# The norm stage of a decoder layer: normed rows multiplied one step later, with g read from PSUM

## The chip, the cores and the metric

The kernel runs on one core of one Trainium2 chip. The metric is device time in microseconds (us): 1281.83 us is the median of three runs of the kernel before (1281.49 to 1283.53). Below, a number such as 586.76 beside an instruction is its start, counted in us from the start of the profiled span.

## What is computed

One hybrid decoder layer on x of 1024 rows by 1024 columns, all in float32. After two groups of attention heads the layer does this, and the change lies in these lines (and in the first norm, which uses the same helper):

```
x = x + einsum('bse,ed->bsd', mixed, w_out)      # output projection and residual
h = rms_norm(x, ffn_norm_g)                      # x * rsqrt(mean(x*x) + eps) * g, row by row
g = einsum('bsd,df->bsf', h, w_gate)
u = einsum('bsd,df->bsf', h, w_up)
x = x + einsum('bsf,fd->bsd', silu(g) * u, w_down)
return rms_norm(x, final_norm_g)
```

Each float32 product is made of three TensorE products of "high" and "low" parts, so every operand is split: ScalarE (ACT) writes the rounded high part, and VectorE (DVE) or GpSimd (POOL) writes the rest, the low part. The gate and up products are made by a Strassen scheme (seven block products in place of eight) on 2 by 2 blocks, which needs sums of blocks of h (named T1 to T4 beside the plain blocks 11, 12, 21, 22) and sums of weight blocks (s1, s2 and two more).

## The kernel before

The 1024 rows are eight row tiles of 128. The stage that the change touches is the loop over `order = (7, 6, 5, 4, 0, 1, 2, 3)` (L812 to L843), the **norm stage**; it lies between the attention and the gate and up products, and step n treats row tile order[n]. It stands in a block whose order is written out by hand: within `manual_schedule` TensorE (PE), DVE, ACT and POOL take their instructions in program order. The DMA queue of SyncE (SP) and all that lies outside the block is ordered by a planner, from its own estimates of time, when the program is built, and the planner may put such instructions between those of the block.

One step n of the loop, engine by engine in program order:
- PE: twelve matmuls of the output projection for columns 0 to 511 (L602, called from L819, tile pso), the transposes of the normed rows of step n - 2 (L757; eight for the lower rows 4 to 7, four for the upper rows), then twelve matmuls for columns 512 to 1023.
- DVE: the residual sum of the first half (L823); the subtractions of step n - 2 on the transposed rows (L765 or L774 into a temporary place, L748 for the low part); in four of the steps the low part of a weight sum (L710, "ol<-temps"); the residual sum of the second half (L823); then the mean of squares plus eps (L136, one column); then the normed rows, x times r times g (L830, tile xn, 1024 columns).
- ACT: copies and high parts of step n - 2 (L762, L744, L764), the high part of a weight sum (L709), the sum of squares of the new rows (L135, with its accumulator read).
- POOL: the power of minus one half (L137, one column), the low part of T3 of step n - 2 (for the upper rows: the subtraction of L779 and the low part of T1), then weight sums by `plan` (L724, L805, L807).

So in the old order L830 of step n stands on DVE after L137 of step n and ahead of the first sum of step n + 1. There is one tile of two temporary places, `temps`: place 0 for T3 or T1, place 1 for weight sums; below the loop both serve T4. The vector g (`gb2`) lies in SBUF, repeated over the 128 partitions. The transposes take their PSUM banks in turn from two pools of two banks, ps_p ("pj") and ps_t ("t").

Below the loop, still by hand (L862 to L882, here **the tail**): four products whose operands are ready, kept in PSUM (`held`), with the transposes of row tiles 2 and 3 and the second column halves of row tiles 0 to 3 between them, and the splits of all these (`first_half`, `first_half_below`). The block ends there. The first product of the stage behind it is `strassen_first`'s product of a11 with block 11 (L957, matmuls on L855, "pst<-11h,oh"), which takes a bank of ps_p. One bank of ps_p is held by the last of the four held products until later.

`rstd_of` (L133 to L138) is also called for each of the eight row tiles of the first norm, at the start of the kernel (0 to 42 us).

## Time and profile before

| | us |
|---|---|
| median of three runs | 1281.83 |
| the profiled execution, its own time | 1281.52 |
| its span | 1279.8 |
| PE busy | 1230.0 (96%) |
| DVE busy | 865.0 (68%) |
| ACT busy | 572.2 (45%) |
| POOL busy | 715.0 (56%) |

The profile is one execution. Each engine takes its instructions in order; a time in brackets behind an instruction is how long the engine sat idle before it, with the engine and the line that ended the wait by the semaphores (of several, the one named can be the wrong one). A matmul row of 0.39 us starts some 0.23 us after the one before it: matmuls overlap. The granted TensorE clock is a share of 2.4 GHz, so 0.50 is its lower level, 1.2 GHz.

### The profile page before, as it was taken

To read this page: it belongs to the slowest core of one execution; us is meant where nothing else is said; L and a number is where in the kernel's file an instruction comes from. 1 tells how busy PE (TensorE), PEld (TensorE's weight loads), DVE (VectorE), ACT (ScalarE), POOL (GpSimd) and SP (SyncE) were. 2 spreads that over 40 slices of the span, in tenths; PEclk is the share of its full clock that TensorE was granted. 3 is DMA by queue.
4 is the path that set the end of the run, shared out by engine and by line. 5 is a ranking of instruction groups with operands and counts; after the bars stand their busy time and mean duration, and the time that the engine had idled before them with its cause. 6 is when DMAs were issued, how large, how long until landed. Compare 5 with 4: busy or idle time off the path is not lost.

```text
span 1279.8 us, 18426 instructions
## 1 busy us (share of the span) xinstructions
PE 1230.0 (96%) x6341; PEld 1043.5 (82%) x6341; DVE 865.0 (68%) x1625; ACT 572.2 (45%) x1209; POOL 715.0 (56%) x653
## 2 busy tenths in 40 slices
PE   8999999999999998988699999999999999999997
PEld 7889988987898877876477888888888887788886
DVE  6456767757786778766666655665665668878765
ACT  4345555646684765534443322333332335534334
POOL 2322333233114353344638777778787758999973
PEclk9999999999999998999899999999999999999999
DMA  6231222132103324122123443223333357645313
GB/s 215 69 102 42 71 76 76 30 93 55 42 5 83 107 87 169 46 99 83 33 68 105 155 142 107 88 97 97 122 107 107 99 179 244 220 124 173 100 58 132
DMA packets 93373, 131.42 MB, mean 103 GB/s; under 512 B 7584, under 2 KB 56288, under 8 KB 93280
## 3 DMA queue, kind: packets, MB, share of 16 engines
q1 hardware_dynamic: 91984, 126.32, 31.7%
q10 hardware_dynamic: 1296, 3.94, 0.8%
q8 instruction: 50, 0.82, 0.3%
q14 instruction: 43, 0.35, 0.1%
HBM read 93.75 MB, written 30.18 MB: 97 GB/s over the span
## 4 chain that ended last, share of the span: by engine, by line
PE 79%; POOL 7%; DVE 5%; issue 4%; ACT 2%; DMA 2%; SPq 0%; POOLq 0%; ACTq 0%; DVEq 0%
PE pst L855 31%; PE psd L1076 13%; PE psv L230 6%; PE pv L375 4%; PE pso L602 3%; PE tp L390 3%; PE s L330 2%; PE s L331 2%; POOL unit L1047 1%; PE psq_f1q L293 1%; PE psq_d2q L293 1%; PE psq_f2q L293 1%; PE psq_d3k L293 1%; PE psq_f1k L293 1%; PE psq_f3q L293 1%
## 5 line engine op out<-in xcount | busy, mean ns | idle before, releaser
L1076 PE MATMUL psd<-unit 128*128 128x512 f32 x924 | 212.5, 392 | 3.9 <-DVE x L1088 3.1
L1076 PEld LDWEIGHTS psd<-unit 128*128 128x128 f32 x924 | 174.1, 189 | 42.1 <-DVE x L1088 3.6
L1047 DVE TENSOR_TENSOR unit<-araw,unit 128x512 fp32r<-128x512 f32 x77 | 104.2, 1380 | 32.1 <-ACT unit L1046 20.3
L710 DVE TENSOR_TENSOR ol<-st,oh 128x512 fp32r<-128x512 f32 x84 | 90.7, 1081 | 50.4 <-ACT oh L709 49.1
L709 ACT CAST oh<-st 128x512 fp32r<-128x512 f32 x84 | 51.1, 620 | 152.3 <-POOL st L724 112.5
L334 ACT ACTIVATE pt<-pt,mn 128x896 f32<-128x896 f32 (+7 forms) x128 | 99.4, 777 | 40.3 <-DVE mn L332 38.2
L397 DVE TENSOR_TENSOR pl<-tp,ph 128x512 fp32r<-128x512 f32 (+1 forms) x120 | 75.3, 633 | 45.2 <-ACT ph L396 44.6
L396 ACT CAST ph<-tp 128x512 fp32r<-128x512 f32 (+1 forms) x120 | 64.2, 542 | 63.9 <-PE tp L390 54.1
L978 POOL TENSOR_TENSOR sg<-sg,cc 128x512 f32<-128x512 f32 x44 | 64.9, 1477 | 44.0 <-ACT sg L977 32.6
L710 DVE TENSOR_TENSOR ol<-raw,oh 128x512 fp32r<-128x512 f32 x66 | 66.8, 1013 | 33.1 <-ACT oh L709 33.0
L1046 ACT CAST unit<-araw 128x512 fp32r<-128x512 f32 x77 | 47.4, 620 | 75.0 <-PE psd L1076 33.9
L422 POOL TENSOR_SCALAR_AFFINE_SELECT cb<-cb 128x128 f32<-128x128 f32 x64 | 22.1, 347 | 99.2 <-DVE mn L332 60.6
L984 POOL TENSOR_TENSOR sg<-sg,cc 128x512 f32<-128x512 f32 x40 | 59.4, 1485 | 29.6 <-DVE cc L983 29.5
L709 ACT CAST oh<-raw 128x512 fp32r<-128x512 f32 x66 | 40.8, 618 | 76.3 <-PE pst L855 74.7
L724 POOL TENSOR_TENSOR st<-raw 128x512 f32<-128x512 f32 x42 | 55.4, 1320 | 31.9 <-DMA raw<-in_w_gate_dram 23.0
L394 POOL MEMSET ph<- 128x128 f32 x48 | 9.9, 207 | 106.2 <-PE pv L375 99.8
L390 PE MATMUL tp<-ident,pt 128*128 128x128 f32 x432 | 67.7, 275 | 0.8 <-DVE pt L475 0.4
L127 POOL TENSOR_TENSOR wl<-wr,wh 128x1024 fp32r<-128x1024 f32 x26 | 63.5, 2445 | 1.4
L126 POOL TENSOR_SCALAR wh<-wr 128x1024 fp32r<-128x1024 f32 x26 | 28.8, 1110 | 52.2 <-PE psq_f2k L293 13.1
L390 PEld LDWEIGHTS tp<-ident,pt 128*128 128x128 f32 x432 | 51.7, 142 | 5.8 <-DVE pl L397 1.4
L230 PE MATMUL psv<-wh,hh 128*128 128x256 f32 x192 | 55.0, 287 | 0.1
L230 PE MATMUL psv<-wl,hh 128*128 128x256 f32 x192 | 54.7, 285 | 0.0
(385 smaller groups left out, 3859.8 us busy)
## 6 DMA issues: line engine op xcount, KB each, us to landing
araw<-act_d SPq DMA_DIRECT2D x77, 256.0 KB, 2.7
raw<-in_w_gate_dram SPq DMA_DIRECT2D x24, 512.0 KB, 3.8
raw<-in_w_up_dram SPq DMA_DIRECT2D x24, 512.0 KB, 3.9
wr<-in_w_in_dram SPq DMA_DIRECT2D x22, 512.0 KB, 4.1
act_d<-sa SPq DMA_DIRECT2D x44, 256.0 KB, 2.5
wraw<-in_w_down_dram SPq DMA_DIRECT2D x40, 256.0 KB, 4.3
act_d<-sg SPq DMA_DIRECT2D x33, 256.0 KB, 2.0
xt<-in_x_dram SPq DMA_DIRECT2D x8, 512.0 KB, 5.0
```

The costliest lines, as they stand in the source:

```text
L230: T.matmul(ps[:, :n], hslice(l, dt, tb), r, start=(k == 0), stop=(k == 23))
L293: T.matmul(ps, l[:, dt], r[half][dt // 4][:, dt % 4], start=(k == 0), stop=(k == 23))
L334: A.activation(pt[:, :L], pt[:, :L], AF.Exp, bias=mn[:, nb - 1:nb], scale=-1.0, accum_out=mn[:, 2:3])
L390: T.transpose(tp[:, a * 256 + b * P:a * 256 + (b + 1) * P], pts[b][:, sb * P:(sb + 1) * P], ident)
L396: A.copy(ph[:, o:], tp[:, o:])
L397: V.tensor_sub(pl[:, o:], tp[:, o:], ph[:, o:].bitcast(F32))
L709: A.copy(h, src)
L710: V.tensor_sub(l, src, h.bitcast(F32))
L855: T.matmul(ps, l[:, j], r[:, j], start=(k == 0), stop=(k == 11))
L978: G.tensor_mul(sg, sg, g)
L1047: lo = le.tensor_tensor(u[:, 2 * k + 1], src, u[:, 2 * k].bitcast(F32), ALU.subtract)
L1076: T.matmul(open_banks[i, m], l, r, start=(k == 0 and not top), stop=(k == last), skip_group_check=top)
```

## The change

- `rstd_of`: the mean of squares times 1/D plus eps moves from DVE (`tensor_scalar`) to ACT (`activation` with Copy, scale and bias). This holds for both norms.
- g is copied once, by two ACT copies, into two PSUM banks: one of the pool ps_v (its only one), one of the two of ps_t. The SBUF place of `gb2` then goes to a second tile of two temporary places.
- The normed rows of step n are no longer written at the end of step n but in step n + 1, on DVE behind the first residual sum, as two instructions of 512 columns that read g from PSUM (`normed`). Those of row tile 3 are written in the tail.
- T3 and T1 alternate between places 0 and 2, T4 between 1 and 3.
- The transposes take ps_p, ps_t, ps_p in turn: three banks. The transposes of row tiles 2 and 3 in the tail take ps_t, ps_p where they took ps_t, ps_p by a cycle of three.
- `plan` and the reload of the first weight blocks move one step later (steps 1 to 6 and 7, for 0 to 5 and 6). The SP loads that belong to them follow the same program places.

```
--- before.py
+++ after.py
@@ -133,7 +133,7 @@
     def rstd_of(src, junk, pool):
         ss = pool.tile([P, 2], F32, tag="ss", name="ss", bufs=4)
         A.activation(junk, src, AF.Square, accum_out=ss[:, 0:1])
-        V.tensor_scalar(ss[:, 0:1], ss[:, 0:1], 1.0 / D, EPS, ALU.mult, ALU.add)
+        A.activation(ss[:, 0:1], ss[:, 0:1], AF.Copy, scale=1.0 / D, bias=EPS)
         rstd_of.last = G.tensor_tensor(ss[:, 1:2], ss[:, 0:1], mhalf, ALU.pow)
         return ss[:, 1:2]
 
@@ -731,10 +731,11 @@
     b_op, xns = {}, {}
     r12, r22 = (fa.tile([P, 4, 512], F32, tag="xb", name=f"r{q}2") for q in (1, 2))
     b_op["T3"] = tuple(fa.tile([P, 4, 512], F32R, tag="xb", name="T3" + c) for c in "hl")
-    temps = bp.tile([P, 2, 512], F32, tag="b", name="temps")
+    temps = [bp.tile([P, 2, 512], F32, tag="b", name="temps")]
 
     def temp(k):
-        return temps[:, k].rearrange("p (j t) -> p j t", j=4)
+
+        return temps[k // 2][:, k % 2].rearrange("p (j t) -> p j t", j=4)
 
     def at(x, t):
         c = t % 4 * P
@@ -749,7 +750,7 @@
 
     turn = [0]
 
-    def transposed(t, q, banks=((ps_p, "pj"), (ps_t, "t"))):
+    def transposed(t, q, banks=((ps_p, "pj"), (ps_t, "t"), (ps_p, "pj"))):
         pool, tag = banks[turn[0] % len(banks)]
         turn[0] += 1
         pt = pool.tile([P, 512], F32, tag=tag, name="pt")
@@ -762,28 +763,30 @@
         A.copy(at(r12, t), pvs[0])
         hi_part("22", t, pvs[1])
         A.copy(at(r22, t), pvs[1])
-        V.tensor_sub(temp(0), pvs[1], at(r12, t))
+        t3 = temp(t % 2 * 2)
+        V.tensor_sub(t3, pvs[1], at(r12, t))
         lo_part("22", t, pvs[1], V)
-        hi_part("T3", t, temp(0))
-        return lambda: lo_part("T3", t, temp(0), G)
+        hi_part("T3", t, t3)
+        return lambda: lo_part("T3", t, t3, G)
 
     def first_half(t, pvs):
 
 
         hi_part("11", t, pvs[0])
-        V.tensor_sub(temp(0), at(r12, t), pvs[0])
+        t1 = temp(t % 2 * 2)
+        V.tensor_sub(t1, at(r12, t), pvs[0])
         lo_part("11", t, pvs[0], V)
-        hi_part("T1", t, temp(0))
+        hi_part("T1", t, t1)
 
         def pool():
-            G.tensor_sub(at(r22, t), at(r22, t), temp(0))
-            lo_part("T1", t, temp(0), G)
+            G.tensor_sub(at(r22, t), at(r22, t), t1)
+            lo_part("T1", t, t1, G)
             hi_part("T2", t, at(r22, t))
         return pool
 
     def first_half_below(t, pv):
 
-        t4 = temp(t % 2)
+        t4 = temp(t % 2 * 2 + 1)
         hi_part("21", t, pv)
         V.tensor_sub(t4, pv, at(r22, t))
         lo_part("21", t, pv, V)
@@ -807,8 +810,21 @@
             G.tensor_tensor(temp(1), a11, a21, ALU.subtract)
 
 
-    plan = {0: (0, 0), 1: (0, 1), 2: (0, 2), 3: (1, 0), 4: (1, 1), 5: (1, 2)}
+    plan = {1: (0, 0), 2: (0, 1), 3: (0, 2), 4: (1, 0), 5: (1, 1), 6: (1, 2)}
     order = (7, 6, 5, 4, 0, 1, 2, 3)
+
+    g_at = [pool.tile([P, 512], F32, tag=tag, name="g_at") for pool, tag in ((ps_v, "pv"), (ps_t, "t"))]
+    for nh in range(2):
+        A.copy(g_at[nh], gb2[:, nh * 512:nh * 512 + 512])
+    temps.append(bp.tile([P, 2, 512], F32, tag="b", name="temps"))
+    rs = {}
+
+    def normed(tb):
+        for nh in range(2):
+            cs = slice(nh * 512, nh * 512 + 512)
+            V.scalar_tensor_tensor(xns[tb][:, cs], x2[tb // 2][:, tb % 2, cs], rs[tb], g_at[nh],
+                                   ALU.mult, ALU.mult)
+
     manual = tc.manual_schedule(engines=NORM_MAN)
     manual.__enter__()
     for n, tb in enumerate(order):
@@ -821,13 +837,15 @@
                 t = order[n - 2]
                 pvs = [transposed(t, q) for q in range(2 if t >= 4 else 1)]
             V.tensor_add(xt[:, cs], ps, xa_half(tb, nh))
-            if nh == 0 and n >= 2:
-                late = (second_half if t >= 4 else first_half)(t, pvs)
-            if nh == 0 and plan.get(n - 1, (0, 0))[1]:
-                early[plan[n - 1][0]].append(operand(temp(1)))
+            if nh == 0:
+                if n >= 1:
+                    normed(order[n - 1])
+                if n >= 2:
+                    late = (second_half if t >= 4 else first_half)(t, pvs)
+                if plan.get(n - 1, (0, 0))[1]:
+                    early[plan[n - 1][0]].append(operand(temp(1)))
         xns[tb] = pp.tile([P, D], F32, tag="p", name="xn")
-        r = rstd_of(xt, xns[tb], sm)
-        V.scalar_tensor_tensor(xns[tb], xt, r, gb2, ALU.mult, ALU.mult)
+        rs[tb] = rstd_of(xt, xns[tb], sm)
         if tb >= 4:
             nc.scalar.dma_start(out=x2_d[(tb - 4) * P:(tb - 3) * P, :], in_=xt)
         if n >= 2:
@@ -836,11 +854,11 @@
             early_sum(*plan[n])
         if n == 1:
             b_op["22"] = big("h22h"), big("h22l")
-        if n == 6:
-            w_first[0] = w_blocks(0, 0)
         if n == 5:
             for name in ("11", "T1", "T2"):
                 b_op[name] = tuple(big(name + c) for c in "hl")
+        if n == 7:
+            w_first[0] = w_blocks(0, 0)
 
 
 
@@ -863,6 +881,7 @@
         b_op[name] = tuple(big(name + c) for c in "hl")
     held[0][0] = product(early[0][0], "22", SS)
     pvs = [transposed(2, 0)]
+    normed(3)
     first_half(2, pvs)()
     held[0][1] = product(early[0][1], "T3", SS)
     pvs = [transposed(3, 0)]
@@ -875,7 +894,7 @@
     for t in (0, 1):
         first_half_below(t, pvs[t])
     held[1][1] = product(early[1][1], "T3", PJ)
-    pvs = [transposed(t, 1, (TT, TT, PJ)) for t in (2, 3)]
+    pvs = [transposed(t, 1, (TT, PJ)) for t in (2, 3)]
     a_first.append(operand(w_first[0][2]))
     for t in (2, 3):
         first_half_below(t, pvs[t - 2])
```

## Rows read from the trace of the kernel before

**Rows 1.** The page: the span, and the busy time of the engines.
```profile
span 1279.8 us, 18426 instructions
PE 1230.0 (96%) x6341; PEld 1043.5 (82%) x6341; DVE 865.0 (68%) x1625; ACT 572.2 (45%) x1209; POOL 715.0 (56%) x653
```
**Rows 2.** Busy time by stretch: the stretch and its length, then PE, PE's weight loads, DVE, ACT, POOL (with counts), the granted clock of PE, the DMA share, GB/s. The first stretch is most of the loop, the second the tail.
```profile
570.00:613.00 43.00, 36.85 (x176) 28.46 (x174) 29.69 (x39) 16.89 (x32) 22.38 (x18) 1.00 0.21 66
613.00:642.00 29.00, 17.93 (x75) 13.68 (x74) 19.30 (x25) 13.90 (x25) 18.93 (x14) 0.83 0.09 30
```
**Rows 3.** The timeline of PE from 586 to 642 us, the rows in which it had waited and the last matmul of the loop: start, length, instruction, count, and in brackets the idle time before it and who ended it.
```profile
586.98 1.06 PE L757 MATMUL pt<-ident,xn 128*128 128x128 f32 x8 [1.40 <-DVE xn L830]
...
595.02 1.06 PE L757 MATMUL pt<-ident,xn 128*128 128x128 f32 x8 [1.44 <-DVE xn L830]
...
612.93 0.39 PE L602 MATMUL pso<-w2h,mx 128*128 128x512 f32 x1
...
617.83 0.63 PE L757 MATMUL pt<-ident,xn 128*128 128x128 f32 x4 [1.35 <-DVE xn L830]
...
625.20 0.79 PE L757 MATMUL pt<-ident,xn 128*128 128x128 f32 x4 [3.77 <-DVE xn L830]
...
636.00 1.94 PE L757 MATMUL pt<-ident,xn 128*128 128x128 f32 x8 [2.23 <-DVE 21l L748]
641.49 0.76 PE L855 MATMUL pst<-11h,oh 128*128 128x512 f32 x1 [3.56 <-ACT T4h L744]
```
**Rows 4.** The timeline of DVE over one step of the loop (n = 3), from its first residual sum to that of the next step.
```profile
586.76 0.68 DVE L823 TENSOR_TENSOR x<-pso,x 128x512 f32<-128x512 f32 x1
587.36 0.67 DVE L765 TENSOR_TENSOR temps<-pt,r 128x512 f32<-128x512 f32 x1
...
589.25 0.69 DVE L710 TENSOR_TENSOR ol<-temps,oh 128x512 fp32r<-128x512 f32 x1 [0.61 <-ACT oh L709]
589.85 0.68 DVE L823 TENSOR_TENSOR x<-pso,x 128x512 f32<-128x512 f32 x1
591.76 0.15 DVE L136 TENSOR_SCALAR ss<-ss 128x1 f32<-128x1 f32 x1 [1.22 <-ACT xn L135]
592.57 2.31 DVE L830 SCALAR_TENSOR_TENSOR xn<-x,ss,gb 128x1024 f32<-128x1024 f32 x1 [0.66 <-POOL ss L137]
594.80 0.68 DVE L823 TENSOR_TENSOR x<-pso,x 128x512 f32<-128x512 f32 x1
```
**Rows 5.** The timelines of ACT and of POOL in the same step.
```profile
588.60 0.62 ACT L709 CAST oh<-temps 128x512 fp32r<-128x512 f32 x1
591.54 0.19 ACT L135 ACTIVATION_READ_ACCUMULATOR xn<-x 128x1 f32 x1
591.63 0.57 ACT L762 COPY r<-pt 128x512 f32<-128x512 f32 x1
...
591.99 0.55 POOL L137 TENSOR_TENSOR ss<-ss,mhalf 128x1 f32<-128x1 f32 x1 [4.01 <-DVE ss L136]
592.51 1.29 POOL L748 TENSOR_TENSOR T3l<-temps,T3h 128x512 fp32r<-128x512 f32 x1
593.75 2.27 POOL L724 TENSOR_TENSOR st<-raw 128x512 f32<-128x512 f32 x1
```
**Rows 6.** The timelines of PE, POOL and DVE at the start of the loop. The PE row is the first transposes of the loop, right behind the first twelve matmuls of step n = 2; the second POOL row is the power of step n = 1; L502 and the rows before it belong to the last attention head.
```profile
570.25 0.60 PE L757 MATMUL pt<-ident,xn 128*128 128x128 f32 x4
...
570.38 1.27 POOL L724 TENSOR_TENSOR st<-raw 128x512 f32<-128x512 f32 x1
...
573.03 0.74 POOL L137 TENSOR_TENSOR ss<-ss,mhalf 128x1 f32<-128x1 f32 x1
...
576.21 0.48 DVE L502 SCALAR_TENSOR_TENSOR mix<-o,g,rp 128x256 f32<-128x256 f32 x1 [2.86 <-PE rp L500]
...
577.51 1.28 DVE L830 SCALAR_TENSOR_TENSOR xn<-x,ss,gb 128x1024 f32<-128x1024 f32 x1
578.71 0.68 DVE L823 TENSOR_TENSOR x<-pso,x 128x512 f32<-128x512 f32 x1
```
**Rows 7.** The timelines of DVE and POOL in the tail: the last residual sum of the loop, the low part of a11, the low parts of block 21 for row tiles 2 and 3, and the four low parts of T2.
```profile
620.06 0.68 DVE L823 TENSOR_TENSOR x<-pso,x 128x512 f32<-128x512 f32 x1
...
632.82 1.83 DVE L710 TENSOR_TENSOR ol<-raw,oh 128x512 fp32r<-128x512 f32 x1 [1.98 <-ACT oh L709]
...
640.67 0.68 DVE L748 TENSOR_TENSOR 21l<-pt,21h 128x512 fp32r<-128x512 f32 x1
641.26 1.28 DVE L710 TENSOR_TENSOR ol<-st,oh 128x512 fp32r<-128x512 f32 x2
...
643.67 0.68 DVE L748 TENSOR_TENSOR 21l<-pt,21h 128x512 fp32r<-128x512 f32 x1
...
632.81 5.89 POOL L748 TENSOR_TENSOR T2l<-r,T2h 128x512 fp32r<-128x512 f32 x4
```
**Rows 8.** The first norm: DVE's mean of squares of row tile 1 and POOL's power behind it (timelines), then two links of the chain that ended last, the squares on ACT (with the accumulator read) of two row tiles that follow each other.
```profile
13.23 0.14 DVE L136 TENSOR_SCALAR ss<-ss 128x1 f32<-128x1 f32 x1
13.45 1.50 POOL L137 TENSOR_TENSOR ss<-ss,mhalf 128x1 f32<-128x1 f32 x1 [2.45 <-DVE ss L136]
...
25.67 1.15 ACT xn L135 x2
...
30.21 1.15 ACT xn L135 x2
```

More of the change, by code (lines that the diff above doesn't have):

```diff
@@ L750, in layer, with transposed @@
     turn = [0]
-    def transposed(t, q, banks=((ps_p, "pj"), (ps_t, "t"))):
+    def transposed(t, q, banks=((ps_p, "pj"), (ps_t, "t"), (ps_p, "pj"))):
         pool, tag = banks[turn[0] % len(banks)]
@@ L807, in early_sum, with normed @@
             G.tensor_tensor(temp(1), a11, a21, ALU.subtract)
-    plan = {0: (0, 0), 1: (0, 1), 2: (0, 2), 3: (1, 0), 4: (1, 1), 5: (1, 2)}
+    plan = {1: (0, 0), 2: (0, 1), 3: (0, 2), 4: (1, 0), 5: (1, 1), 6: (1, 2)}
     order = (7, 6, 5, 4, 0, 1, 2, 3)
+    g_at = [pool.tile([P, 512], F32, tag=tag, name="g_at") for pool, tag in ((ps_v, "pv"), (ps_t, "t"))]
+    for nh in range(2):
+        A.copy(g_at[nh], gb2[:, nh * 512:nh * 512 + 512])
+    temps.append(bp.tile([P, 2, 512], F32, tag="b", name="temps"))
+    rs = {}
+    def normed(tb):
+        for nh in range(2):
+            cs = slice(nh * 512, nh * 512 + 512)
+            V.scalar_tensor_tensor(xns[tb][:, cs], x2[tb // 2][:, tb % 2, cs], rs[tb], g_at[nh],
+                                   ALU.mult, ALU.mult)
     manual = tc.manual_schedule(engines=NORM_MAN)
@@ L823, in layer @@
             V.tensor_add(xt[:, cs], ps, xa_half(tb, nh))
-            if nh == 0 and n >= 2:
-                late = (second_half if t >= 4 else first_half)(t, pvs)
-            if nh == 0 and plan.get(n - 1, (0, 0))[1]:
-                early[plan[n - 1][0]].append(operand(temp(1)))
+            if nh == 0:
+                if n >= 1:
+                    normed(order[n - 1])
+                if n >= 2:
+                    late = (second_half if t >= 4 else first_half)(t, pvs)
+                if plan.get(n - 1, (0, 0))[1]:
+                    early[plan[n - 1][0]].append(operand(temp(1)))
         xns[tb] = pp.tile([P, D], F32, tag="p", name="xn")
-        r = rstd_of(xt, xns[tb], sm)
-        V.scalar_tensor_tensor(xns[tb], xt, r, gb2, ALU.mult, ALU.mult)
+        rs[tb] = rstd_of(xt, xns[tb], sm)
         if tb >= 4:
@@ L843, in layer @@
                 b_op[name] = tuple(big(name + c) for c in "hl")
+        if n == 7:
+            w_first[0] = w_blocks(0, 0)
     def product(a, name, at=None):
@@ L865, in layer @@
     pvs = [transposed(2, 0)]
+    normed(3)
     first_half(2, pvs)()
@@ L877, in layer @@
     held[1][1] = product(early[1][1], "T3", PJ)
-    pvs = [transposed(t, 1, (TT, TT, PJ)) for t in (2, 3)]
+    pvs = [transposed(t, 1, (TT, PJ)) for t in (2, 3)]
     a_first.append(operand(w_first[0][2]))
```

26 lines of the change are left out of this document (13 added, 13 removed).

## The prediction

> **What bounds the kernel now.** I read the page first: PE is busy for 96% of the span [rows 1], so only a stretch where PE stands still can give much. The table by stretches shows one: between 570 and 642 us PE is busy for 36.85 of 43 us and for 17.93 of 29 us, some 17 us idle, and in the second part its clock is at 0.83 on the mean [rows 2]. The timeline of PE says for what: from step to step its transposes wait for the normed rows of L830, in the tail for L830 again and for the splits of block 21 [rows 3]. Two of these rows lie 8.04 us apart (586.98 and 595.02), 1.44 of it idle, so PE's own step is 6.60.
>
> DVE's step is the 8.04 [rows 4]: five operations that follow each other every 0.60 (586.76 to 587.36), and between them 0.61 for ACT's high part, 1.22 for the squares, L136, 0.66 for the power, and L830 with 2.23 until the next start. L830 lasts 2.31 there and 1.28 where POOL rests [rows 4, 6]: it starts at 592.57 while POOL's T3l runs (592.51 to 593.80), and POOL's next sum then takes 2.27 where another took 1.27 [rows 5, 6]. They take turns. The sums at L823 and L765, with one operand in PSUM, stay at 0.68.
>
> DVE is also late from the start. PE's first matmuls of step 2 are done at 570.25, their sum on DVE runs at 578.71, 8.4 later [rows 6]: ahead of it in the queue stand L830 of step 1 (577.51), whose power ran at 573.03 behind weight sums, and L502 of the last head (576.21). At the end of the loop DVE is still 6.7 behind: the last matmul ends at 613.32, its sum starts at 620.06 [rows 3, 7]. So the stage's end is set by DVE with ACT and POOL in its loop, and not by PE.
>
> **The change, part by part.** The *normed rows a step later* take 1.22, 0.66, L136 and 2.23 off the end of DVE's step and put two operations of 512 columns, with one operand in PSUM, behind the first sum. The nearest rows are L823 and L765, so 2 x 0.60 = 1.20; the other end is the old 2.23, if they too took turns with POOL. I take 1.20, since those rows keep 0.68 while POOL works. DVE then has 5 x 0.60 + 1.20 + 0.61 = 4.8 of work in a step.
>
> What is late next? PE needs 6.60. The loop through POOL: second sum 0.68, squares and their read until 591.73 (1.20 behind the sum's end at 590.53), 0.26 to the power, power 0.52, T3l 1.24, weight sum 1.25, its high part 0.67, its low part 0.64 [rows 4, 5]: 6.46. The loop through the normed rows: the same 2.66 to the power's end, 1.20, T3's subtraction 0.60, its high part 0.71, the other high part 0.53, the low part 0.64: 6.3. Three loops end within 0.3 of each other; I take PE's 6.60 (bounds 6.5, and 7.6 if the multiplication stays at 2.23). The multiplication now waits for the power in front of step n - 2's subtractions and the second sum on DVE; that is why its loop is counted here. PE is not hurt by the later rows: they are ready 1.9 behind the first sum of one step and asked for by the transposes of the next, 6.6 later, some 4 us of slack.
>
> *Mean of squares on ACT.* No row of this stage shows a one-column activation that follows the read. The nearest is the read itself, 0.19 [rows 5]; with two hops of 0.04 the power starts 0.27 after it, as now (0.26). Bounds 0.1 less and 0.5 more in each step. ACT is held for 0.23 more; in the loop it has more idle time than that. In the *first norm* it has not: the squares of two row tiles follow each other by 4.54 on the chain (25.67 and 30.21), through ACT, so four such links cost 0.9. Against that, the power of row tile 1 no longer waits for DVE's queue (13.23), nor runs for 1.50 against DVE's split beside it [rows 8]; that brings the next squares some 1.1 forward. Together 0 (bounds -1.1 and +1.9).
>
> *Weight sums a step later, g copied, places.* Power 1 no longer stands behind the sums of 570.38, so L823 of step 2 can run at 570.9 in place of 578.71. The bound on the other side is 576.8, if L502 stays ahead of it. The two g copies are about 0.6 each (as ACT's 0.57 [rows 5]) in ACT's idle time, costing nothing if their bank is free in time. The reload on SP waits for the sum of step 6, which ends at about 608 (second sum 601.2, 2.66, three operations of 1.25); its reader comes 10 us behind the second sum of step 7, so the load has 11 us, and 0 to 2 us are lost if that does not cover it. Four places take away DVE's waits for POOL's low parts.
>
> *The sum to the last residual sum.* From 570.9 five steps of 6.60 give the first sum of step 7 at 603.9. PE would allow the second at about 606.8. But POOL has one operation more in steps 6 and 7 (L779), and the weight sum of step 6 is split in step 7, so its loop is 6.46 + 1.25 = 7.7 from the second sum of step 6 (597.3 + 3.9 = 601.2): 608.9. I take 609.0 against 620.06: **-11.0**.
>
> *The tail.* Now the first product behind it starts 21.43 after that sum (641.49). In the new order: 2.66 to the power's end, five POOL operations of 1.25 to the subtraction of row tile 3, 1.2 for two high parts on ACT: 10.1; the low part of a11, two operands in SBUF, then waits for one T2l and ends at 12.0 (now 14.6, [rows 7]). But here a bank is missed. The old product started 0.14 after block 21's low part of row tile 2 (640.67 + 0.68 = 641.35); the row names ACT, which writes no operand of it. In the new turn that free bank of ps_p goes to row tile 3, whose low part comes 3.0 later (643.67), 1.2 of it two splits that the planner put between. So 6.7 behind a11 becomes 8.5 to 9.7, and the tail is 20.6 to 21.8: what POOL's places give, the bank takes back. I take 0.
>
> All behind 641 then moves forward by 11.0, since PE is nearly without gaps there. 1281.52, the profiled execution's own time (span 1279.8), less 11.0 is 1270.5; the median lies 0.3 above that execution, so 1270.8.
>
> **Rule against row.** L823 shows 0.60 for 512 columns from PSUM, and L830 alone 1.20 for 1024 columns from SBUF (577.51 to 578.71) [rows 4, 6]: no difference. The Trainium skill, "Perfetto Trace Analysis", section "Optimizing Scalar/DVE Operations", gives DVE about 125 ns of overhead on PSUM and 60 on SBUF, which speaks against two halves from PSUM: 0.19 more per row tile, 1.5 in all. The rows do not show it, and with DVE at 4.8 of 6.6 the sum would stay. Its section "Matmul Optimizations" asks that all eight PSUM banks be put to use; parking g in two speaks against that, and rival C is what this would do here.
>
> **The rivals.** *B, the start stays late.* L502 waited 2.86 for PE, and the planner lays it. If it stays ahead of step 2's sum, or a g copy waits for a bank of ps_t until the last head is done, that sum runs at 576.8. Then 576.8 + 33.0 + 5.1 = 614.9, only 5.2 gained: 1276.6. For it: DVE's loops are as long as PE's, so lateness is not made good. Against: the old order put L830 ahead, which is gone.
>
> *C, the missing bank binds harder.* With one bank in ps_t the transposes of row tile 2 wait for the low part of row tile 1, not 0, some 2.9 later, and the product for row tile 3, 3.0 later. If both lie on the path, the tail is 5.9 longer: 1276.7. For it: PE did wait there (2.23, 3.56). Against: DVE has other splits to do meanwhile.
>
> *D, slower: the last head's block arrives late.* The output projection needs that head's rows for row tile 0, in step 4 at about 581. Its transposes share the single bank of ps_t with step 2's, whose readers come after the normed rows on DVE. If the planner lets three more steps go first, PE stands still for 3 x 6.6 = 19.8 in the loop: 1290.6. The point from which it decides is 11 us of standing still, a block later than 592. Against: now L502 makes it at 576.21 [rows 6], 15 us ahead of that point.
>
> *B and C together, or a change that does nothing*, would be 1279.3 to 1284.4.
>
> **How the numbers follow.** Forecast 0.60 (1267.5 to 1274.5, from the bounds of step and tail); more gained, with the low clock in the tail gone too, 0.05; B 0.15; C 0.08; neutral 0.06; D 0.06. A measurement here can tell 0.2%, 2.6 us, from no change. Faster 0.60 + 0.05 + 0.15 + 0.08 = 0.88, same 0.06, slower 0.06. The range takes in the forecast, B and C: 1266 to 1279.
>
> **What would show it.** DVE's step at 6.5 to 6.7, its multiplication as two rows of 0.68 whatever POOL does; step 2's first sum at about 571; the last residual sum at about 609; the first product of block 11 at about 630, right behind row tile 3's low part of block 21. It is wrong if the first sum stays near 577 (B), if the first product comes more than 23 us behind the last residual sum (C), or if PE waits in step 4 (D).

## The result and the profile after

The kernel after takes 1270.04 us (median of four runs, 1268.52 to 1270.63) against 1281.66 for the kernel before beside it (four runs, 1278.91 to 1283.53): the ratio is 0.9909, 95% interval 0.9889 to 0.9929. It is faster, by 0.9%; the prediction said 1270.8. The same kernel run again beside the second group of experiments gave 0.9929 (0.9906 to 0.9952). The profiled execution took 1268.52, its span 13.0 less than that of [rows 1].

The page of the kernel after, span and engines:

```profile
span 1266.8 us, 18426 instructions
PE 1222.2 (96%) x6341; PEld 1039.2 (82%) x6341; DVE 857.3 (68%) x1617; ACT 576.1 (45%) x1227; POOL 710.5 (56%) x653
```

The same two stretches as in [rows 2], with the same columns. PE is busy for 4.3 more in the first, where it hardly waits any longer, and its clock in the second is 0.88 where it was 0.83 (the second stretch holds later work than before, since all came forward):

```profile
570.00:613.00 43.00, 41.15 (x203) 34.18 (x204) 28.70 (x45) 23.91 (x49) 23.48 (x23) 1.00 0.25 86
613.00:642.00 29.00, 20.39 (x86) 16.23 (x85) 20.19 (x29) 15.61 (x27) 11.55 (x9) 0.88 0.18 55
```

To compare like with like, take in each kernel the stretch from the first residual sum of the loop on DVE to the first matmul behind the tail, with the same columns, before and then after:

```profile
557.41:641.49 84.08, 66.86 (x312) 52.31 (x311) 54.66 (x76) 34.00 (x65) 42.84 (x34) 0.95 0.17 58
554.90:628.96 74.06, 62.65 (x312) 51.44 (x311) 46.85 (x77) 37.56 (x75) 37.01 (x34) 0.98 0.19 65
```

PE does the same 312 matmuls in both. Of the 10.0 that went, 5.8 is idle time of PE (17.2 to 11.4) and 4.2 is busy time, at a mean clock of 0.98 in place of 0.95; so not all of it is waiting.

The timeline of PE: first the transposes of the loop, then the last matmul of the loop's projections (604.30), then the waits of the tail and the first matmuls behind it. It answers to [rows 3].

```profile
570.46 0.63 PE L758 MATMUL pt<-ident,xn 128*128 128x128 f32 x4 [1.32 <-DVE xn L825]
...
582.74 1.03 PE L758 MATMUL pt<-ident,xn 128*128 128x128 f32 x8
...
589.07 1.03 PE L758 MATMUL pt<-ident,xn 128*128 128x128 f32 x8
...
604.30 0.39 PE L602 MATMUL pso<-w2h,mx 128*128 128x512 f32 x1
...
612.02 0.63 PE L758 MATMUL pt<-ident,xn 128*128 128x128 f32 x4 [1.40 <-DVE xn L825]
...
628.96 0.80 PE L873 MATMUL pst<-21h,oh 128*128 128x512 f32 x1 [6.25 <-DVE ol L710]
629.56 0.63 PE L873 MATMUL pst<-T2h,oh 128*128 128x512 f32 x1
...
634.36 0.40 PE L873 MATMUL pst<-11h,oh 128*128 128x512 f32 x1
```

Within the loop no row carries a bracket after 570.46: PE waits no more, and its step is 6.33 (582.74 to 589.07). The first work behind the tail is no longer a11's product but one matmul on 21h and then T2's product.

One step of DVE (n = 4), then ACT and POOL in it, against [rows 4, 5]. Two rows of L839 as "x2" are the second sum of one step and the first of the next.

```profile
584.88 1.41 DVE L825 SCALAR_TENSOR_TENSOR xn<-x,ss,g_at 128x512 f32<-128x512 f32 x2 [1.25 <-POOL ss L137]
586.20 0.69 DVE L767 TENSOR_TENSOR temps<-pt,r 128x512 f32<-128x512 f32 x1
...
588.09 0.69 DVE L710 TENSOR_TENSOR ol<-temps,oh 128x512 fp32r<-128x512 f32 x1 [0.61 <-ACT oh L709]
588.70 1.28 DVE L839 TENSOR_TENSOR x<-pso,x 128x512 f32<-128x512 f32 x2
591.46 1.41 DVE L825 SCALAR_TENSOR_TENSOR xn<-x,ss,g_at 128x512 f32<-128x512 f32 x2 [1.48 <-POOL ss L137]
```

```profile
590.38 0.19 ACT L135 ACTIVATION_READ_ACCUMULATOR xn<-x 128x1 f32 x1
590.60 0.20 ACT L136 ACTIVATE ss<-ss 128x1 f32<-128x1 f32 x1
...
590.88 0.55 POOL L137 TENSOR_TENSOR ss<-ss,mhalf 128x1 f32<-128x1 f32 x1 [3.52 <-DMA raw<-in_w_up_dram]
591.39 1.30 POOL L749 TENSOR_TENSOR T3l<-temps,T3h 128x512 fp32r<-128x512 f32 x1
592.65 1.29 POOL L724 TENSOR_TENSOR st<-raw 128x512 f32<-128x512 f32 x1
```

The multiplication runs beside T3l and the weight sum, and all three keep their lengths: 1.41, 1.30, 1.29, where [rows 4, 5] have 2.31 for one and 2.27 for the other. DVE stands still 1.2 to 1.5 ahead of it in such a step; it is no longer the bound.

The start on ACT, POOL and DVE (answers to [rows 6]):

```profile
562.38 0.58 ACT L818 COPY g_at<-gb 128x512 f32<-128x512 f32 x1
...
568.35 0.58 ACT L818 COPY g_at<-gb 128x512 f32<-128x512 f32 x1
...
572.41 0.55 POOL L137 TENSOR_TENSOR ss<-ss,mhalf 128x1 f32<-128x1 f32 x1 [4.18 <-ACT ss L136]
572.92 1.30 POOL L724 TENSOR_TENSOR st<-raw 128x512 f32<-128x512 f32 x1
...
563.03 0.74 DVE L825 SCALAR_TENSOR_TENSOR xn<-x,ss,g_at 128x512 f32<-128x512 f32 x1
...
568.27 0.48 DVE L494 TENSOR_SCALAR dg<-ones,rr 128x128 f32<-128x128 f32 x2 [0.27 <-POOL rr L492]
...
569.57 0.74 DVE L825 SCALAR_TENSOR_TENSOR xn<-x,ss,g_at 128x512 f32<-128x512 f32 x1
570.23 1.28 DVE L839 TENSOR_TENSOR x<-pso,x 128x512 f32<-128x512 f32 x2
```

The second sum of the pair, 570.83, is the first of step 2. The second copy of g comes so late that the second half of row tile 7 is multiplied 6.5 behind the first. ACT had stood idle for 5.08 before the L507 of attention that runs just ahead of that copy (568.04); whether the copy's bank or its place in ACT's order held it is not shown.

The tail on DVE and POOL (answers to [rows 7]):

```profile
608.36 0.69 DVE L839 TENSOR_TENSOR x<-pso,x 128x512 f32<-128x512 f32 x1
...
620.05 0.69 DVE L710 TENSOR_TENSOR ol<-raw,oh 128x512 fp32r<-128x512 f32 x1 [1.96 <-ACT oh L709]
...
628.29 1.28 DVE L710 TENSOR_TENSOR ol<-st,oh 128x512 fp32r<-128x512 f32 x2
...
630.70 0.68 DVE L749 TENSOR_TENSOR 21l<-pt,21h 128x512 fp32r<-128x512 f32 x1
...
620.06 5.96 POOL L749 TENSOR_TENSOR T2l<-r,T2h 128x512 fp32r<-128x512 f32 x4
```

**Where the 13.0 of the profile lie.** Call the stretch from the first residual sum of the loop on DVE to the first matmul behind the tail the *stage*: 84.08 before and 74.06 after, as shown above. So 10.0 came from the stage, 2.5 lie ahead of it and 0.5 behind. Ahead of it PE has the same work in both kernels. By 440 us both profiles stand at the same time; 1.9 of the 2.5 come between 476 and 498 us. What differs there is the granted clock, between 480 and 500 us 0.83 before and 1.00 after (windows, columns as in [rows 2]); before:

```profile
480.00:490.00 10.00, 7.27 (x42) 6.67 (x43) 8.07 (x24) 6.83 (x22) 6.31 (x10) 0.83 0.91 358
```

and after:

```profile
480.00:490.00 10.00, 6.48 (x48) 5.84 (x48) 9.65 (x24) 7.27 (x23) 6.30 (x10) 1.00 0.96 369
```

Among all profiles of this study the first residual sum starts between 553.2 and 558.6, in kernels with the same attention. The comparisons below therefore go by the stage's length as well as by the time. The stage's length is not free of the clock either: from the first to the second residual sum, in the same work, the profiles need 2.7 to 3.9.

### The profile page after: what moved, and what is told of

Same layout as the page of the kernel before. It is cut to its first block, busy times and chain, and to the rows that moved or that the text cites. A ratio compares the mean times of both kernels' runs of the same rounds, so it can differ in the third digit from the quotient of the medians.

```text
span 1266.8 us, 18426 instructions
## 1 busy us (share of the span) xinstructions
PE 1222.2 (96%) x6341; PEld 1039.2 (82%) x6341; DVE 857.3 (68%) x1617; ACT 576.1 (45%) x1227; POOL 710.5 (56%) x653
## 4 chain that ended last, share of the span: by engine, by line
PE 81%; POOL 6%; DVE 5%; issue 3%; DMA 3%; ACT 2%; SPq 0%; POOLq 0%; ACTq 0%; DVEq 0%
PE pst L873 31%; PE psd L1095 14%; PE psv L230 6%; PE pso L602 4%; PE pv L375 4%; PE tp L390 3%; PE s L330 2%; PE s L331 2%; POOL unit L1066 2%; POOL tw L1050 1%; PE psq_f1q L293 1%; PE psq_d2q L293 1%; PE psq_f2q L293 1%; PE psq_d3k L293 1%; PE psq_f1k L293 1%
## 5 line engine op out<-in xcount | busy, mean ns | idle before, releaser
L126 POOL TENSOR_SCALAR wh<-wr 128x1024 fp32r<-128x1024 f32 x26 | 27.8, 1069 | 52.3 <-PE psq_f2k L293 13.8
```

## The experiments

Ratios are to the kernel before, timed on the same chip in the same group of runs; its medians were 1283.65 (for rows in their own step, g in SBUF in one instruction, weight sums early and two places), 1281.51 (for after again, g in SBUF in two halves, first row tile from SBUF and product in the tail) and 1281.33 (for the other four). A ratio is not exactly the quotient of the two medians; where the runs of a kernel spread unevenly the two differ. "Sums" is the first residual sum to the last, "tail" from there to the first matmul behind it, "stage" both, all from the one profile of each kernel.

| kernel | us | ratio (95%) | sums | tail | stage |
|---|---|---|---|---|---|
| before | 1281.66 | 1 | 62.65 | 21.43 | 84.08 |
| after | 1270.04 | 0.9909 (0.9889 to 0.9929) | 53.46 | 20.60 | 74.06 |
| after, again | 1271.83 | 0.9929 (0.9906 to 0.9952) | 53.61 | 20.60 | 74.21 |
| rows in their own step | 1274.86 | 0.9938 (0.9920 to 0.9955) | 57.34 | 20.80 | 78.14 |
| g in SBUF, one instruction | 1284.40 | 1.0009 (0.9994 to 1.0024) | 63.70 | 21.91 | 85.61 |
| g in SBUF, two halves | 1287.95 | 1.0043 (1.0031 to 1.0055) | 67.14 | 21.80 | 88.94 |
| weight sums early | 1274.43 | 0.9930 (0.9917 to 0.9944) | 56.23 | 20.85 | 77.08 |
| two places | 1273.12 | 0.9918 (0.9900 to 0.9936) | 53.28 | 20.91 | 74.19 |
| first row tile from SBUF | 1274.73 | 0.9939 (0.9924 to 0.9954) | 55.83 | 20.82 | 76.65 |
| only that one from PSUM | 1281.73 | 1.0008 (0.9994 to 1.0023) | 64.27 | 21.81 | 86.08 |
| g in PSUM alone | 1275.39 | 0.9971 (0.9956 to 0.9985) | 58.45 | 20.98 | 79.43 |
| mean on DVE, second norm | 1271.62 | 0.9927 (0.9913 to 0.9940) | 53.45 | 20.82 | 74.27 |
| mean on DVE, first norm | 1269.98 | 0.9915 (0.9902 to 0.9929) | 53.82 | 20.60 | 74.42 |
| product in the tail | 1270.36 | 0.9912 (0.9898 to 0.9926) | 53.10 | - | - |

By the time alone only four of these kernels are clearly slower than the kernel after: the two with g in SBUF, only that one from PSUM, and g in PSUM alone. The intervals of all others overlap with those of the kernel after; what is said of them below rests on the stage in one profile each.

**After, again.** No edit.

> The changed kernel itself, unaltered, as the mark for the three beside it and as a test of where its 13 us of one profile came from. Theory (only the stage behind attention became shorter, by some 10 us; attention merely differs from one execution to the next): ratio to the kernel before 0.990 to 0.992, and in its profile the stretch from the first residual sum to the first product behind the tail is again within 0.5 us of 74.1 (554.90 to 628.96 in the first profile), while the first residual sum itself may lie anywhere from 554.9 to 557.9. Rival (the change shortens attention too): the first residual sum lies again near 554.9.

The stage came out at 74.21, 0.15 from the first profile; the ratio, 0.9929, lies a little above the range expected. But the first residual sum lay at 554.07, near the first profile's, as the rival has it. So what the stage gained repeats to 0.15; on the 2.5 ahead of it see the end of the next section. Both profiles of the kernel after are of the fastest of its runs timed beside them (here 1268.58, the median being 1271.83), so they show it at its best.

**Rows in their own step.**

```diff
-                if n >= 1:
-                    normed(order[n - 1])
...
         rs[tb] = rstd_of(xt, xns[tb], sm)
+        normed(tb)
...
-    normed(3)
     first_half(2, pvs)()
```

> The changed kernel with one part undone: each row tile is multiplied at the end of its own step again, right behind its power, still with g from PSUM and the mean of squares on ACT. My theory: the step was 8.04 because of two waits (1.22 and 0.66) and a multiplication of 2.23 on DVE; g in PSUM alone takes the last to 1.2 to 1.4, so the step becomes about 7.0 with a weight sum and stays near PE's 6.3 without one, and the first sum of step 2 comes 3 later, behind the multiplication of row tile 6. Last residual sum 2 to 4 later than in the changed kernel (608.4): 1272 to 1274 against 1270.0. Rival: the delay by a step is the whole of it, the step goes back to 8 and the time to 1278 or more. Second rival: PE's own order hides it, 1270.

4.0 more in the stage. By the two ratios it is 3.7 more than the first timing of the kernel after (0.0029 of 1281.66) but only 1.2 more than the second (0.0009), inside the intervals, so the time does not confirm the size. DVE then waits for its own row tile's power in every step, and the next step's first sum stands behind it:

```profile
587.45 1.41 DVE L825 SCALAR_TENSOR_TENSOR xn<-x,ss,g_at 128x512 f32<-128x512 f32 x2 [2.08 <-POOL ss L137]
...
594.64 1.41 DVE L825 SCALAR_TENSOR_TENSOR xn<-x,ss,g_at 128x512 f32<-128x512 f32 x2 [2.08 <-POOL ss L137]
595.96 0.68 DVE L839 TENSOR_TENSOR x<-pso,x 128x512 f32<-128x512 f32 x1
...
600.52 1.41 DVE L825 SCALAR_TENSOR_TENSOR xn<-x,ss,g_at 128x512 f32<-128x512 f32 x2 [2.08 <-POOL ss L137]
```

A step is 7.19 with a low part of a weight sum and 5.88 without; DVE is the bound.

**g in SBUF, one instruction.** `normed` as `V.scalar_tensor_tensor(xns[tb], x2[...], rs[tb], gb2, ...)`, without copies of g and with two places.

> The changed kernel with g read from SBUF in one instruction of 1024 columns per row tile; the two copies of g and the second tile of temporary places are gone with it (their SBUF place is g's), the transposes keep their turn. My theory: the multiplication starts together with POOL's low part of T3 and takes turns with it, so it lasts 2.2 to 2.3 again and POOL's next sum 2.2; both loops of 6.3 to 6.5 become about 7.4, longer than PE's step: last residual sum about 5 later, 1274 to 1277. Rival: DVE has enough idle time in a step and the turns are absorbed, 1270 to 1271.5; it would even gain a little, since nothing waits for a copy of g at the start.

Worse than either expected: nothing is left of the gain. The multiplication is back at 2.30 beside POOL (584.36, 591.87, 599.36: steps of 7.5), and the start is late besides, PE having waited 3.30 at 572.04 for pieces of the last attention head. DVE, then PE:

```profile
584.36 2.31 DVE L819 SCALAR_TENSOR_TENSOR xn<-x,ss,gb 128x1024 f32<-128x1024 f32 x1 [1.49 <-POOL ss L137]
```

```profile
572.04 0.40 PE L500 MATMUL rp<-ident,dg 128*128 128x128 f32 x1 [3.30 <-DVE dg L494]
```

Two causes in one run. The trace parts them roughly: from the second residual sum of step 2 to the last, behind the late start, it takes 37.46, against 38.25 before and 32.85 after. So the loop itself gains only 0.8 by the new order while the turns last. The next three runs part them further.

**g in SBUF, two halves.** As the kernel with two places, and in `normed`:

```diff
-    g_at = [pool.tile(...) for pool, tag in ((ps_v, "pv"), (ps_t, "t"))]
-    for nh in range(2):
-        A.copy(g_at[nh], gb2[:, nh * 512:nh * 512 + 512])
...
-            V.scalar_tensor_tensor(xns[tb][:, cs], x2[...], rs[tb], g_at[nh],
+            V.scalar_tensor_tensor(xns[tb][:, cs], x2[...], rs[tb], gb2[:, cs],
```

> As the run with two temporary places (1273.12 us, 0.9918), with g read from SBUF in place of PSUM and without the two copies of g; the multiplication stays in two instructions of 512 columns, in the same written order. Theory (turns between VectorE and GpSimd make the step long): each half takes about twice 0.6 while a GpSimd piece runs beside it and the piece as long, so the steps with a weight sum go from 6.33 to about 7.5, as with the one instruction of 1024 columns: over four such steps some 4 to 5 us, 1277 to 1279 us, ratio 0.995 to 0.997. Rival (the loss of 11 us with one instruction of 1024 columns came from the order at the start alone, where VectorE stood 5.54 for the last pieces of attention): steps stay at 6.3 to 6.6 and the time within 1 us of 1273.

It came out slower than before: 14.8 more in the stage than with two places alone. The theory's direction holds, its size does not. DVE, then POOL:

```profile
595.26 3.44 DVE L821 SCALAR_TENSOR_TENSOR xn<-x,ss,gb 128x512 f32<-128x512 f32 x2 [1.49 <-POOL ss L137]
```

```profile
595.18 1.29 POOL L749 TENSOR_TENSOR T3l<-temps,T3h 128x512 fp32r<-128x512 f32 x1
596.43 1.72 POOL L810 TENSOR_TENSOR temps<-raw 128x512 f32<-128x512 f32 x1
```

Two halves are two turns: the first stands behind T3l, the second behind the weight sum, which itself stood behind the first. So 3.45 in place of 2.30 for one instruction, and the step is 8.64 (586.62 to 595.26). Of the 14.8, 1.0 lies between the first two residual sums (3.91 against 2.90), where the matmuls ran 0.43 apart until 560.5; that is not the edit's.

**First row tile from SBUF.** All as after, but `normed` takes `gb2[:, cs]` where n is 1.

> The first row tile behind attention reads g from SBUF, all others from PSUM; all else as in the changed kernel. It takes away the wait of the second half of that row tile for the second copy of g (idle of 3.47 on VectorE up to 569.57). Theory (from 576 on TensorE's own 6.33 a step and its first products set the pace, and the first residual sum of step 2 waits for TensorE at 570 anyway): the time changes by 0 to -1 us against the changed kernel beside it. Rival (that wait delays the whole chain): -2 to -3 us.

Both fell: it is 2.4 longer in the stage than the kernel after beside it (76.65 against 74.21) and 2.9 slower by the medians, though the intervals of the ratios overlap. PE and its clock, then POOL, then DVE:

```profile
571.36 0.30 PE L500 MATMUL rp<-ident,dg 128*128 128x128 f32 x1 [1.29 <-DVE dg L494]
572.47 0.33 PE L500 MATMUL rp<-ident,dg 128*128 128x128 f32 x1 [0.81 <-DVE dg L494]
573.37 0.85 PE L758 MATMUL pt<-ident,xn 128*128 128x128 f32 x4 [0.57 <-DVE mix L502]
```

```profile
574.00:578.00 4.00, 4.00 (x14) 3.14 (x13) 1.60 (x3) 1.94 (x4) 0.00 (x0) 0.61 0.00 0
```

```profile
569.66 1.27 POOL L724 TENSOR_TENSOR st<-raw 128x512 f32<-128x512 f32 x1
571.01 1.32 POOL L724 TENSOR_TENSOR st<-st,raw 128x512 f32<-128x512 f32 x1
```

```profile
564.48 1.40 DVE L825 SCALAR_TENSOR_TENSOR xn<-x,ss,gb 128x512 f32<-128x512 f32 x2
...
570.93 1.49 DVE L494 TENSOR_SCALAR dg<-ones,rr 128x128 f32<-128x128 f32 x2
```

Row tile 7 is done at once, at 564.48. The weight sums on POOL then run at 569.66, beside the last head's L494 on DVE (1.49 for two, 0.48 after), and PE stands for 1.29, 0.81 and 0.57, in all 2.7, for that head, where the kernel after waits 1.32. L494 also starts later here, since the first sum of step 2 (569.67) and half a multiplication (570.27) stand ahead of it on DVE. Behind these waits the granted clock fell, 0.61 from 574 to 578: the twelve matmuls behind the transposes take 4.35 (573.87 to 578.22) where the kernel after needs 2.84 (570.84 to 573.68). So the longer wait and the low clock, 1.4 and 1.5, share the loss; that the wait made the clock fall is not shown. In the kernel after the weight sums run at 572.92, when the head's pieces are through. The late copy of g is no loss: behind it the new stage's work came after attention's last pieces.

**Only that one from PSUM.** The reverse: row tile 7 from PSUM, the other seven from SBUF, two places.

> The counterpart of the run whose first row tile alone read g from SBUF: here the first row tile behind attention alone reads g from PSUM, the seven others read it from SBUF; two temporary places, order as written in the changed kernel. Theory (two costs add: where g's two PSUM banks are held, attention's last pieces come ahead of the new stage's work, which is worth 2.6; and from there on VectorE and GpSimd take turns, with steps of 8.6 with a weight sum and 7.3 without against 6.33): the first residual sum to the last takes 53.3 plus 11.3 (67.14 with all row tiles from SBUF less 55.83 with the first alone), 64.6, the first product follows 21.8 later at 86.4, and the ratio is 1.000 to 1.003. Rival (the start is late because of the turns themselves): the stage is as long as with all eight from SBUF, 88.9, ratio 1.004.

The theory held to 0.4: sums 64.27, stage 86.08, ratio 1.0008; its first transposes wait 1.32 at 568.42 as in the kernel after, and its steps are 8.62 to 8.66 and 7.33 to 7.37. Turns in the loop cost 11.9 over the stage with two places; reading row tile 7 from SBUF too costs 2.9 on top of that (88.94). Of these, 1.2 lie between the first two residual sums, where only the clock differs; the rest, 1.7, is of the order of the 2.4 above.

**Weight sums early.** `plan` begins at step 0 and the reload stands at `n == 6`, as before.

> The changed kernel with the weight sums (and the reload of the first blocks) one step earlier, as before the change. My theory after the trace of the changed kernel: the power of row tile 6 there runs at 572.4 behind its own squares (a copy of g held DVE until 569.6), not behind sums, so the sums in front of it would have been done by 571 and cost at most 1; at the end the split of the last sum leaves step 7, where POOL's extra operation made DVE wait, which gives back up to 1.2. Together 1269 to 1270.5. Rival, as I forecast: the sums in front of the power are a main part of the late start, the first sum of step 2 goes to 575 to 577 and the time to 1274 to 1276.

The theory missed, the rival is nearer: 3.0 more in the stage, though by the ratio it is level with the second timing of the kernel after. The weight sums run at 572.04 and 573.38, beside L494 and L508 of the last head, which take 1.48 each; the second half of row tile 7 comes 8.4 behind the first, and PE waits 1.08 and 2.22. It is the same collision as above:

```profile
572.11 1.48 DVE L494 TENSOR_SCALAR dg<-ones,rr 128x128 f32<-128x128 f32 x2 [0.27 <-POOL rr L492]
```

Here too the clock fell behind the waits (0.66 from 578 to 582; the twelve matmuls take 4.42 for 2.84), and 0.9 more lies between the first two residual sums. In one part the theory was right: from the first to the last residual sum of step 7 it is 5.22 against 6.82, so 1.6 came back at the end.

**Two places.**

> The changed kernel with two temporary places instead of four. My theory: with the multiplication between them, DVE's subtraction of a step comes behind POOL's low part of the step before anyway, and in the tail the subtraction of row tile 3 waits for ACT's high part of block 11 as long as for the place: 0 to 0.5 more, 1270 to 1270.5. Rival, from my forecast of the tail: the places are worth 2.6 there, 1272.5.

The edit puts T3 and T1 on place 0 alone and T4 on places 0 and 1. Stage 74.19, no different from after; the time lies 0.0009 higher, inside both intervals. The waits for POOL's T1l in the tail (1.1) are where the kernel after waits for ACT's high part of 11 (0.97 to 1.0). Four places are worth 0.3 in the tail (20.91 against 20.60) and 0.1 or nothing in the stage.

**g in PSUM alone.** The kernel before with `normed` in two halves from PSUM at the old place in the order, and the banks of the transposes that this needs.

> The kernel before with nothing but g read from PSUM, in two instructions of 512 columns in each row tile's own step (and the banks of transposed tiles that this needs); mean of squares on VectorE, weight sums and their reload at the old steps, two temporary places. Theory (the parts add: the stage is 78.1 with the normed rows in their own step and 3.0 more with the sums at the old steps): 81.1 from the first residual sum to the first product against 84.08 before, ratio 0.997 to 0.999. Rival (the turns were the whole loss, and the earlier sums cost only where the row is multiplied a step later): 78 to 79, ratio 0.994 to 0.995.

Neither theory is settled. The ratio is as the theory has it, but the quotient of the medians is 0.9954, near the rival's: seven of twelve runs lie at 1274.1 to 1275.5, five at 1278.0 to 1282.5. The stage, 79.43, lies between the two, nearer the rival's 78 to 79 than the theory's 81.1. It has the collision at the start as well (PE waits 1.07 and 2.22; the twelve matmuls behind take 4.45). The start, to the first sum of step 2, stays at 21.56 (21.30 before), and the rest of the loop goes from 41.35 to 36.89: that is what the turns cost there. So 4.65 of 10.0 come from PSUM alone; from there to the kernel with rows in their own step (later sums, mean on ACT, four places) it is 1.3, where the early sums alone cost 3.0 with the rows a step later.

**Mean on DVE, second norm; and first norm.** `V.tensor_scalar(ss, ss, 1.0 / D, EPS, ...)` in the one or the other.

> The changed kernel with the mean of squares of the second norm on VectorE again; the first norm's stays on ScalarE. Theory (VectorE stands idle for 1.0 to 2.1 ahead of most multiplications, waiting for GpSimd's power, so one more instruction of some 0.16 in that gap costs only its own hand-over): the stage stays within 0.6 of 74.1 and the ratio within 0.001 of the changed kernel's. Rival (the mean is queued on VectorE behind pieces of the step, and the power and the multiplication wait for it): steps of 6.6 or more, 2 us or more in all.

> The changed kernel with the mean of squares of the first norm on VectorE again; the second norm's stays on ScalarE. Theory (the first norm is paced by ScalarE, where squares are 4.77 apart in the changed kernel against 4.54 before, the mean's own 0.2 of it): squares 4.54 apart again, the first product of the projections at 46.8 in place of 47.3, and 0 to -0.5 us in all, which the timing can't tell from none. Rival (the mean on ScalarE starts the power earlier): 0 to +1 us.

Stages of 74.27 and 74.42, within the theories; ratios 0.9927 and 0.9915, the first within 0.001 of the second timing of the kernel after (0.9929), not of the first. With the first norm's mean on DVE the squares are again 4.54 apart (25.52, 30.06), and the first product of the projections starts at 46.47 in place of 47.12. But the links are not what makes it late: the last squares of the norm start at 34.60 here and at 34.55 in the kernel after. There the last multiplication of the norm (L184 on DVE, 37.65) takes 2.02, where it takes 1.28 here and before; POOL's two rows of L126 beside it take 2.06, and 3.04 here and before. They take turns in all three, and with the mean on ACT POOL is 0.2 earlier (36.54 for 36.76) and goes first. All eleven profiles with the first norm's mean on ACT have 2.02 or 2.03, the three without it 1.27 or 1.28. The timing does not tell either kernel from the kernel after.

**Product in the tail.**

```diff
+    first_p1 = product(a_first[0], "11", (ps_v, "pv"))
     pvs = [transposed(t, 1, (TT, PJ)) for t in (2, 3)]
...
-            A.copy(p1, product(a_first[0] if m == 0 else operand(a11), "11"))
+            A.copy(p1, product(operand(a11), "11") if m else first_p1)
```

> The first product of the block multiplication (a11 times b11 of the first group) is made within the tail, in the PSUM bank that held g's first half, where TensorE stands idle for 6.25 us; all else as in the changed kernel. Theory (the tail's end is set by VectorE's and GpSimd's chain, TensorE has idle time for this product's 2.8 us, and the products behind start as before): -1.5 to -2.8 us against the changed kernel beside it. Rival (its operands, the low parts of the last row tiles of block 11, come so late that the product stands ahead of others in TensorE's queue): 0 or slower.

Not shown to be faster: 1.5 less by the medians, intervals that overlap, and from the first residual sum to the end of the span 713.7 against 712.8. The product is made where it was put, but the idle time stays:

```profile
620.83 0.50 PE L873 MATMUL pst<-11h,ol 128*128 128x512 f32 x1 [0.30 <-DVE ol L710]
...
629.69 0.77 PE L873 MATMUL pst<-T1h,oh 128*128 128x512 f32 x1 [5.42 <-ACT T4h L745]
```

The planner laid T1's product next, and PE waits 5.42 for it where it waited 6.25 for 21h and T2's.

## Why the prediction came out

The time was right within 0.8 us. By its own terms:

| term | predicted | measured |
|---|---|---|
| first norm | 0 | +0.5 to the first product (46.63 to 47.12), 0.0 by 440 us |
| attention | 0 | -2.5 |
| first residual sum to first sum of step 2 | 21.30 to 13.49 | 15.93 |
| from there to the last residual sum | 41.35 to 38.1 | 37.53 |
| tail | 21.43 | 20.60 |
| stage | -11.06 | -10.02 |
| behind | 0 | -0.5 |

The predicted values go by clock times less 557.41, so 570.9 is 13.49. The sum at 570.83 looks like a hit on 570.9, but that clock time has attention's 2.5 in it: the start gained 5.4, not 7.8. The profile came out 2.0 below the 1270.5 foreseen for it, the median 1.5 above the profile; part of the agreement is that the mis-sized start and the 2.5 have opposite signs.

*Turns between DVE and POOL.* Right, and the centre of the case: with one operand in PSUM they are gone, and without that the new order gains nothing (stage 85.61, part of it the late start; 0.8 in the loop behind that). Part of the step was mis-sized. The multiplication takes 1.41 for its two rows, 1.32 from start to start, not 1.20; the first, 0.74, was priced by L823's 0.68. And PE's step is 6.33, not 6.60: a bracket counts from the end of a matmul of 0.39, but without a wait the next would have started 0.23 after it, so 0.16 of the 0.27 was the reading's.

*Rule against row.* Two halves from SBUF with POOL at rest take 1.40 in the run with the first row tile from SBUF, two from PSUM 1.41. What makes 1.41 out of 1.28 is the second instruction, not PSUM; the 0.19 more per row tile, an estimate from what the Trainium skill ("Perfetto Trace Analysis", section "Optimizing Scalar/DVE Operations") gives for PSUM, is not there.

*The rows a step later.* Right in the stage: 4.0. Their worth hangs on the turns being gone, which the prediction added as if they were two separate terms. It treated the change as a sum, and the runs show an interaction: g in PSUM alone 4.65, all but g in PSUM -1.5, both 10.0. The first two have the low clock behind their late starts in them (4.45 and 4.04 for the twelve matmuls that take 2.84); taken out, 6.3 and -0.3, they still do not add up to 10.0.

*The start.* The step that failed in its reason, and the term that was mis-sized most: 5.4 for 7.8. The prediction had the gain from power 1 no longer standing behind weight sums. [rows 6] speak against that: the power was done at 573.77, and L830 of step 1 started at 577.51, behind L502, which waited 2.86 for PE. In the runs the weight sums matter, but because their turns slow attention's last pieces, for which PE then waits, with the clock lower for some 4 us behind the wait (3.0 in the stage with sums early, 2.4 with the first row tile from SBUF). Nor do the later sums bring it alone: the start takes 20.33 with the rows in their own step, 18.68 with the sums early and 15.93 with both moved. That a g copy might wait for a bank was named in rival B, as a loss; a late second copy was there, 5.97 behind the first, whatever held it, and the runs in which row tile 7 did not stand behind it have the longer stage.

*The tail.* The price was nearly right, 0.8 too long, for a wrong reason. Places were to give 2.6 and a missing bank to take it back. Places give 0.3, and a11's low part came early for another cause: it started 0.01 ahead of T2l and met no turn (0.69 against 1.83). It mattered little: in the run with two places it took 1.83 again, and the tail was 20.91. The missing bank was not met, since the planner put T2's product first; that waits for the low part of s2 (628.29), itself laid behind block 21's splits on DVE. The product of a11 starts at 634.36, behind row tile 3's low part of block 21 (630.70 + 0.68) and behind T2's matmuls, which ran 0.43 apart after 6.25 of idle. That is 26.0 behind the last residual sum; read to the letter, the sign that names the first product of block 11 would have spoken for rival C, but the planner's order and not the bank made it late. (In the kernel before row tile 2 took the bank of ps_p there and row tile 3 that of ps_t, the reverse of the order after; the list of the change has the same order for both.)

*Mean on ACT.* 0, as predicted, and the power starts 0.31 behind the read's end (590.57 to 590.88), 0.04 more than foreseen: its two hops are 0.03 and 0.08, as in [rows 4, 5], and not 0.04 each. In the first norm the four links of 0.23 are there (4.77 against 4.54 apart), and the earlier first squares more than made them good (last squares at 34.55, 34.76 before). What made the first product 0.5 later is L184's turn behind POOL (2.02 for 1.28), which the prediction did not have.

*Rivals.* C and D did not occur. B's mechanism, attention's pieces that come late, is there in five of the experiments, where PE waits 2.7 to 3.3 at the seam for 1.3 in the kernel after: both with g in SBUF, weight sums early, first row tile from SBUF, g in PSUM alone.

**The 2.5 ahead of the stage.** They need not be the change's. In the run with g in PSUM alone, whose program ahead of the loop is that of the kernel before, the first residual sum lies at 553.66, ahead of both profiles of the kernel after. The granted clock from 480 to 490 and from 490 to 500 us differs between executions that do the same work there: 0.83 and 0.83 before, 1.00 and 1.00 in both profiles of the kernel after, 0.83 and 1.00 with g in PSUM alone, 1.00 and 0.66 with sums early. Why it falls in some of them is open.

## What to carry to other kernels

Where DVE and POOL both work from SBUF, look for rows that are twice as long beside the other engine as alone: moving one operand of the DVE instruction to PSUM can be worth more than any reordering, and here reordering was worth next to nothing until that was done. Cutting an instruction in halves while the turns last makes it worse. At the seam between two stages ask which stage's last pieces the new work slows; starting the new work early on a side engine can cost the old stage more than it brings. Look also at the clock behind such a wait of PE: in four runs it cost 1.2 to 1.6 more, beside 1.4 to 2.0 of added waiting.

## What the hardware showed that was not expected

- With two operands in SBUF, DVE and POOL do not share, one waits for the whole instruction of the other: 2.30 for one instruction of 1024 columns (1.28 alone), but 3.45 for two of 512 (1.40 alone). The Trainium skill ("SBUF — State Buffer", section "SBUF: two separate sides") has the shared port pair as a lock held for the whole instruction; the two turns of the halves are how that looks in a trace.
- Small pieces suffer more, relative to their length: L494, 0.48 for two of 128 columns, took 1.48 beside a weight sum.
- After 6.25 of idle PE's clock fell to its lower level for a while: T2's matmuls ran 0.43 apart from 629.56 to 633.8, where others run 0.23 apart; the stretch's mean is 0.88.
- At the seam the same happened behind waits of 2.7 to 3.3 in four runs of five (0.61 from 574 to 578 with the first row tile from SBUF), at a cost of 1.2 to 1.6 each. In the fifth, g in SBUF in two halves, PE waited 2.76 at 575.91 and the clock stayed at 1.00, so such a wait does not always bring it.
